# Loads of x for the residual stream tied to SyncE's weight loads, and the transposed x in five parts among the first weights

## The chip, the cores and the metric

The kernel runs on one core of a Trainium2 chip. The metric is the time of one execution on the device in microseconds (us), as the median of several runs. A profile of one execution stands beside it; its rows name the engines PE (TensorE), PEld (its weight loads), DVE (VectorE), ACT (ScalarE), POOL (GpSimd) and SP (SyncE).

## The reference

The kernel computes a decoder trunk of two layers over x, 256 positions by 2048 features, float32. Cut to what the change touches:

```python
def reference(x, ...):
    h = x
    for layer in range(DEPTH):                       # DEPTH = 2
        xn = rms_norm(h, norm_mix[layer])
        if layer % 2 == 0:
            mix = swa_mlstm_mixer(xn, w_in_even[0], w_out_even[0], ...)
        else:
            mix = forgetting_attention_mixer(xn, w_in_odd[0], ...)
        h = h + mix
        h = h + swiglu(rms_norm(h, norm_ffn[layer]), w_gate[layer], w_up[layer], w_down[layer])
    return rms_norm(h, norm_final)

def rms_norm(x, g):
    return x * rsqrt(mean(x * x, axis=-1) + 1e-5) * g

def swa_mlstm_mixer(xn, w_in, ...):
    proj = xn @ w_in                                 # 2048 features to all heads' inputs
    q_s, k_s, v_s, q_m, k_m, v_m, o_m, i_m, f_m = split_cols(proj, EVEN_SIZES)
    ...
```

The row factor rsqrt(mean(x * x) + 1e-5) scales a whole row of `xn`, so the kernel multiplies x times the gain g with the weights and applies the row factor to the product.

## The kernel before

All weights are float32 in DRAM. A product of float32 quality is made of three matmuls in PE's faster float32 form: each operand is split into a rounded part and the rest (`hi` and `lo` of a weight, `xh` and `xl` of x), and hi times xh, lo times xh and hi times xl are added up in PSUM (lines 178 to 180 of `gemm`).

Weights come in chunks: `load_raw` (line 105) issues on SyncE a load of 256 rows by 512 columns, 512 KB, into a tile `raw`, of which there are four buffers. `split_chunk` casts it on ACT into `hi` (line 150) and subtracts on DVE for `lo` (line 151); `hi` and `lo` have six buffers each. A chunk feeds 12 matmuls: two row blocks of 128, two halves of the 256 positions, three products. A raw buffer is free for the next load when `lo` is made.

The order of work at the start is this:

1. x is loaded a first time, transposed on the host, as `xc` (16 tiles of 128 features by 256 positions, 2 MB), in four loads of four tiles (line 115). Among them stand the loads of the first four chunks, kept in the list `ahead`.
2. The first projection, into `acc0`, are the keys and values of the window attention (512 columns at `OFF_KS`): chunks 1 to 8. For each n of four, the scalings of four tiles of `xc` to `xh` (ACT, line 562) and `xl` (DVE, line 563) stand ahead of two chunks.
3. The second projection, into `acc1`, is the first half of the queries: chunks 9 to 16. After every two chunks the kernel loads a quarter of x in its plain layout into `h`, the residual stream (line 573, 512 KB on SyncE), and ACT squares it and adds up the rows (line 201 in `square_sum`, two instructions per quarter, each with a read of the accumulator).
4. `rstd` makes of the sums the row factor `r` (DVE lines 207 and 208, POOL line 210). It is first used to take `acc0` out of PSUM: `kd` on ACT (line 604), `vs` on DVE (line 609). `acc0` and `acc1` hold two PSUM banks each, out of four in their pool; the third projection takes the banks of `acc0`.

The program isn't executed in the order it is written in: a scheduler places the instructions of each engine by its own estimate of times, under the data dependences, and every engine then executes its list in order. `tc.issue_after(ins)` adds an edge to this: what is traced in its block, on the engine of `ins`, is placed behind `ins`. In the loop of the second projection `ins` is `latest[0]`, the last cast on ACT, while the instruction in the block is a load on SyncE:

```python
        with tc.issue_after(latest[0].ins):
            nc.sync.dma_start(h[:, :, n * NB : (n + 1) * NB], xv[:, :, n * NB : (n + 1) * NB])
        square_sum("m0", n)
```

In the built program the head of SyncE's list, which holds all loads of weights, of `xc` and of `h`, reads: `xc` part 1, chunks 1 and 2, `xc` part 2, chunks 3 and 4, `xc` parts 3 and 4, `h` in four parts, chunks 5 to 24. ACT's list reads, from the first scaling on: four scalings, casts 1 and 2, four scalings, casts 3 and 4, eight scalings, eight squares, seven casts, `kd`, a cast, `kd`, casts.

Of the kernel before, what the change touches and what calls it, by code (L numbers as in the profile page):

```python
# [23 lines left out]
NB = 512  # L24
# [7 lines left out]
OFF_QS, OFF_KS = 0, 1024  # L32
# [22 lines left out]
def trunk(  # L55
# [20 lines left out]
    nc = tc.nc  # L76
# [22 lines left out]
    xc = gp.tile([P, KT, S], F32, name="xc")  # L99
    gT = cp.tile([P, 4 * KT], F32, name="gT")  # L100
    nc.scalar.dma_start(gT, gains)

    def load_raw(w, k0, c0, n, pool=wr):
        raw = pool.tile([P, CK, NB], F32, tag="raw", name="raw", bufs=4 if pool is wr else RAWS)
        nc.sync.dma_start(
            raw[:, :, 0:n], w[k0 * P : (k0 + CK) * P, c0 : c0 + n].rearrange("(k p) n -> p k n", p=P)
        )
        return raw

    wi = w_in_even[0]  # L110
    h = cp.tile([P, NT, D], F32, name="h")
    xv = x[0].rearrange("(t p) d -> p t d", p=P)
    ahead = []
    for n in range(4):
        nc.sync.dma_start(xc[:, 4 * n : 4 * n + 4, :], xt[:, 4 * n : 4 * n + 4, :])
        for k in {0: (0, 2), 1: (4, 6)}.get(n, ()):
            ahead.append(load_raw(wi, k, OFF_KS, NB))

    ident = cp.tile([P, P], F32, name="ident")
    nc.gpsimd.memset(ident, 0.0)  # L120
# [20 lines left out]
    latest = [None]  # L141

    def load_chunk(w, k0, c0, n):
        raw = ahead.pop(0) if ahead else load_raw(w, k0, c0, n)
        return split_chunk(raw, n)
# [18 lines left out]
    def gemm(acc, lhs, w, c0, n, k_from, k_to, k_all, skew=1):  # L164
        k0 = k_from
        while k0 < k_to:
            last = k_to == k_all and k0 + skew * CK >= k_all
            chunks = [load_chunk(w, kc, c0, n) for kc in range(k0, k_all if last else k0 + CK, CK)]
            order = [(i, t) for i in range(len(chunks) * CK) for t in range(NT)]
            if last:  # L170
                order.sort(key=lambda it: it[1])
            for i, t in order:
                k = k0 + i
                hi, lo = (c[:, i % CK, 0:n] for c in chunks[i // CK])
                ah, al = lhs(k)
                ts = slice(t * P, (t + 1) * P)
                o = acc[t][:, 0:n]
                nc.tensor.matmul(o, ah[:, ts], hi, start=(k == 0), stop=False)  # L178
                nc.tensor.matmul(o, ah[:, ts], lo, start=False, stop=False)  # L179
                nc.tensor.matmul(o, al[:, ts], hi, start=False, stop=(k == k_all - 1))  # L180
            k0 += len(chunks) * CK
# [14 lines left out]
    def square_sum(key, n):  # L196
        if n == 0:
            sums[key] = sm.tile([P, NT, 4], F32, tag="ss", name="ss")
        for t in range(NT):
            junk = sm.tile([P, NB], BF16, tag="junk", name="junk", bufs=1)  # L200
            nc.scalar.activation(
                junk, h[:, t, n * NB : (n + 1) * NB], AF.Square, accum_out=sums[key][:, t, n : n + 1]
            )
# [160 lines left out]
    def pair_group(fp, par, lhs, sums, mats, order, todo=()):  # L364
# [5 lines left out]
        for pos, (kind, pair) in enumerate(order):  # L370
# [18 lines left out]
            if first:  # L389
                prods = [bank(1 - par, "prod") for _ in range(4)]  # L390
            ra, rb = (load_raw(w, k0, c0, NB, fp) for w, c0 in mats)
            hg, lg = split_chunk(ra, NB)
            run_due(todo, pos)
# [175 lines left out]
    acc1 = new_acc()  # L569
    for n in range(4):  # L570
        gemm(acc1, x_of, wi, OFF_QS, NB, 4 * n, 4 * n + 4, KT)
        with tc.issue_after(latest[0].ins):
            nc.sync.dma_start(h[:, :, n * NB : (n + 1) * NB], xv[:, :, n * NB : (n + 1) * NB])
        square_sum("m0", n)
    r = rstd("m0")
    with tc.tile_pool(name="ev", bufs=1) as ev:
# [22 lines left out]
        with tc.tile_pool(name="sw", bufs=1) as sw:  # L599
# [10 lines left out]
            ks = sw.tile([P, KVH, S], F32, name="ks")  # L610
# [379 lines left out]
```

## Time and profile before

| | us |
|---|---|
| median of 3 runs | 2132.34 |
| lowest and highest | 2132.19, 2133.31 |
| the profiled execution | 2132.55 |
| its span, first to last instruction | 2130.8 |
| PE busy in it | 2108.0 |
| ACT busy, DVE busy | 1252.5, 1709.9 |

The granted clock of PE has a mean of 0.997 over the span. The DMA queues moved 420.95 MB, at a mean of 198 GB/s. Busy time of PE has modelled ends: a matmul of 512 columns is shown with some 0.39 us, and the next one of its kind begins 0.23 us after it.

### The profile page before, as it was taken

What the parts mean: (1) busy time and instruction counts of PE and PEld (TensorE: products, weight loads), DVE (VectorE), ACT (ScalarE), POOL (GpSimd) and SP (SyncE); (2) the same over time, 40 slices, a digit from 0 to 9 for tenths busy, and PEclk for the clock granted to TensorE, in tenths of its full rate; (3) what the DMA queues carried; (4) which work ended last, traced back from release to release, by engine and by line L of the source; (5) the groups of instructions that cost most, each with busy time, mean ns of one, the idle gap of its engine ahead of it and who ended that gap; (6) DMA issues with size and microseconds to landing.
All of it is one profiled execution on the core that took longest, in us unless ns stands there. A gap on an engine that the chain in (4) does not pass through costs nothing.

```text
span 2130.8 us, 26787 instructions
## 1 busy us (share of the span) xinstructions
PE 2108.0 (99%) x9708; PEld 1749.6 (82%) x9708; DVE 1709.9 (80%) x2204; ACT 1252.5 (59%) x1592; POOL 35.7 (2%) x61
## 2 busy tenths in 40 slices
PE   7999999999999999999999999999999999999998
PEld 5888888888888888888888888888888888888886
DVE  5666567899999999999755554668899998999995
ACT  6474456665577655766645444556655667556763
POOL 2010000000000000000000000000000000000000
PEclk9999999999999999999999999999999999999999
DMA  8455556675667666775575664656766767666763
GB/s 290 137 166 151 169 194 197 202 223 171 228 208 217 200 206 204 233 224 179 168 232 166 177 173 141 229 175 186 223 197 210 232 190 207 228 197 205 226 208 131
DMA packets 257845, 420.95 MB, mean 198 GB/s; under 512 B 56448, under 2 KB 64688, under 8 KB 257584
## 3 DMA queue, kind: packets, MB, share of 16 engines
q1 hardware_dynamic: 256832, 415.49, 62.9%
q0 software_dynamic: 736, 3.71, 0.6%
q8 instruction: 76, 1.25, 0.2%
q14 instruction: 57, 0.47, 0.1%
q10 hardware_dynamic: 144, 0.03, 0.0%
HBM read 406.57 MB, written 2.11 MB: 192 GB/s over the span
## 4 chain that ended last, share of the span: by engine, by line
PE 98%; DMA 1%; ACT 1%; DVE 0%; issue 0%; SPq 0%; DVEq 0%; POOLq 0%; POOL 0%; ACTq 0%
PE acc L357 17%; PE acc L358 17%; PE acc L359 17%; PE acc L180 11%; PE acc L178 11%; PE acc L179 10%; PE prod L357 4%; PE prod L358 4%; PE prod L359 4%; PE ptm L264 1%; PE p L281 1%; PE po L332 1%; DMA xc<-in_xt_dram 1%; PE pt L230 0%; PE pp L324 0%; PE p L274 0%
## 5 line engine op out<-in xcount | busy, mean ns | idle before, releaser
L150 ACT CAST hi<-raw 128x1024 fp32r<-128x1024 f32 (+2 forms) x682 | 696.0, 1032 | 584.5 <-PE acc L180 259.0
L151 DVE TENSOR_TENSOR lo<-raw,hi 128x1024 fp32r<-128x1024 f32 (+2 forms) x682 | 810.3, 1200 | 249.8 <-ACT hi L150 248.1
L358 PE MATMUL acc<-lo,xh 128*128 128x512 f32 x946 | 368.1, 389 | 0.0
L357 PE MATMUL acc<-hi,xh 128*128 128x512 f32 x946 | 365.1, 390 | 0.3 <-DVE u L422 0.3
L359 PE MATMUL acc<-hi,xl 128*128 128x512 f32 x946 | 363.2, 389 | 0.0
L178 PE MATMUL acc<-hi,xh 128*128 128x512 f32 (+3 forms) x736 | 276.5, 378 | 12.4 <-ACT hi L150 12.4
L180 PE MATMUL acc<-hi,xl 128*128 128x512 f32 (+3 forms) x736 | 277.2, 378 | 0.0
L179 PE MATMUL acc<-lo,xh 128*128 128x512 f32 (+3 forms) x736 | 276.7, 376 | 0.3 <-DVE lo L151 0.2
L357 PEld LDWEIGHTS acc<-hi,xh 128*128 128x128 f32 x946 | 177.6, 188 | 37.9 <-DVE u L422 1.1
L359 PEld LDWEIGHTS acc<-hi,xl 128*128 128x128 f32 x946 | 177.5, 188 | 37.1
L358 PEld LDWEIGHTS acc<-lo,xh 128*128 128x128 f32 x946 | 177.6, 188 | 36.6
L358 PE MATMUL acc<-lo,mh 128*128 128x512 f32 x444 | 173.1, 390 | 0.0
L359 PE MATMUL acc<-hi,ml 128*128 128x512 f32 x444 | 171.1, 389 | 0.0
L357 PE MATMUL acc<-hi,mh 128*128 128x512 f32 x444 | 170.1, 389 | 0.0
L178 PEld LDWEIGHTS acc<-hi,xh 128*128 128x128 f32 x736 | 139.6, 190 | 36.0 <-ACT hi L150 12.8
L179 PEld LDWEIGHTS acc<-lo,xh 128*128 128x128 f32 x736 | 139.6, 190 | 26.0 <-DVE lo L151 2.2
L180 PEld LDWEIGHTS acc<-hi,xl 128*128 128x128 f32 x736 | 139.5, 190 | 25.8 <-issue 1.9
L252 ACT CAST ht<-raw 128x1024 fp32r<-128x1024 f32 x94 | 98.7, 1050 | 51.8 <-issue 20.8
L253 DVE TENSOR_TENSOR lt<-raw,ht 128x1024 fp32r<-128x1024 f32 x94 | 114.6, 1219 | 16.5 <-ACT ht L252 16.2
L178 PE MATMUL acc<-hi,mh 128*128 128x512 f32 x320 | 125.8, 393 | 1.2 <-ACT mh L252 1.2
L179 PE MATMUL acc<-lo,mh 128*128 128x512 f32 x320 | 125.7, 393 | 0.0
L180 PE MATMUL acc<-hi,ml 128*128 128x512 f32 x320 | 124.0, 390 | 0.0
(307 smaller groups left out, 3071.6 us busy)
## 6 DMA issues: line engine op xcount, KB each, us to landing
raw<-in_w_gate_dram SPq DMA_DIRECT2D x176, 512.0 KB, 4.6
raw<-in_w_up_dram SPq DMA_DIRECT2D x176, 512.0 KB, 4.7
raw<-in_w_down_dram SPq DMA_DIRECT2D x176, 512.0 KB, 4.9
raw<-in_w_in_odd_dram SPq DMA_DIRECT2D x88, 512.0 KB, 3.8
raw<-in_w_in_even_dram SPq DMA_DIRECT2D x64, 512.0 KB, 4.4
raw<-in_w_out_even_dram SPq DMA_DIRECT2D x32, 512.0 KB, 3.7
raw<-in_w_out_odd_dram SPq DMA_DIRECT2D x32, 512.0 KB, 3.9
raw<-in_w_in_odd_dram SPq DMA_DIRECT2D x8, 272.0 KB, 2.9
```

The source lines that it names most:

```text
L150: latest[0] = nc.scalar.copy(hi[:, :, 0:n], raw[:, :, 0:n])
L151: nc.vector.tensor_tensor(out=lo[:, :, 0:n], in0=raw[:, :, 0:n], in1=hi[:, :, 0:n].bitcast(F32), op=ALU.subtract)
L178: nc.tensor.matmul(o, ah[:, ts], hi, start=(k == 0), stop=False)
L179: nc.tensor.matmul(o, ah[:, ts], lo, start=False, stop=False)
L180: nc.tensor.matmul(o, al[:, ts], hi, start=False, stop=(k == k_all - 1))
L252: nc.scalar.copy(dst_h, src)
L253: nc.vector.tensor_tensor(out=dst_l, in0=src, in1=dst_h.bitcast(F32), op=ALU.subtract)
L264: nc.tensor.transpose(pt[:, i, :], s_, ident)
L281: nc.tensor.matmul(p1[:, jj, :], q_of(j, 1), k_of(j), start=True, stop=True)
L357: nc.tensor.matmul(o, ah, hi, start=start, stop=False)
L358: nc.tensor.matmul(o, ah, lo, start=False, stop=False)
L359: nc.tensor.matmul(o, al, hi, start=False, stop=stop)
```

## The change

Two edits at the start of the kernel. `load_raw` now keeps its latest load in `load[0]`, and the loads of `h` name that load, an instruction of SyncE, in `issue_after`. The loads of `xc` become five: two tiles, two, four, four, four; chunk 1 stands behind the first part, chunk 2 behind the second, chunks 3 and 4 behind the third.

```diff
+    load = [None]
+
     def load_raw(w, k0, c0, n, pool=wr):
         raw = pool.tile([P, CK, NB], F32, tag="raw", name="raw", bufs=4 if pool is wr else RAWS)
-        nc.sync.dma_start(
+        load[0] = nc.sync.dma_start(
             raw[:, :, 0:n], w[k0 * P : (k0 + CK) * P, c0 : c0 + n].rearrange("(k p) n -> p k n", p=P)
         )
         return raw
...
     ahead = []
-    for n in range(4):
-        nc.sync.dma_start(xc[:, 4 * n : 4 * n + 4, :], xt[:, 4 * n : 4 * n + 4, :])
-        for k in {0: (0, 2), 1: (4, 6)}.get(n, ()):
-            ahead.append(load_raw(wi, k, OFF_KS, NB))
+    for k0, k1, ks in ((0, 2, (0,)), (2, 4, (2,)), (4, 8, (4, 6)), (8, 12, ()), (12, 16, ())):
+        nc.sync.dma_start(xc[:, k0:k1, :], xt[:, k0:k1, :])
+        ahead += [load_raw(wi, k, OFF_KS, NB) for k in ks]
...
     for n in range(4):
         gemm(acc1, x_of, wi, OFF_QS, NB, 4 * n, 4 * n + 4, KT)
-        with tc.issue_after(latest[0].ins):
+        with tc.issue_after(load[0].ins):
             nc.sync.dma_start(h[:, :, n * NB : (n + 1) * NB], xv[:, :, n * NB : (n + 1) * NB])
         square_sum("m0", n)
```

## The prediction

> **What bounds the kernel now.** I read the windows view first, over stretches that I cut at the idle ends of PE, then PE's waits, then the timeline of the first 34 us, then the landings of single loads.
>
> ```profile
> PE 2108.0 (99%) x9708; PEld 1749.6 (82%) x9708; DVE 1709.9 (80%) x2204; ACT 1252.5 (59%) x1592; POOL 35.7 (2%) x61
> PE acc L178 <- ACT hi L150: 12.4, 2, 7.5
> PE acc L178 <- ACT mh L252: 1.2, 1, 1.2
> 0.00:7.50 7.50, 0.00 (x0) 0.00 (x0) 1.75 (x6) 4.11 (x7) 3.51 (x14) 1.00 0.73 198
> 15.86:21.15 5.29, 5.29 (x22) 4.05 (x22) 4.25 (x9) 5.21 (x14) 0.96 (x3) 1.00 1.05 386
> 21.15:26.07 4.92, 0.00 (x0) 0.00 (x0) 0.54 (x3) 4.76 (x14) 4.50 (x12) 0.88 1.05 393
> 26.07:31.90 5.83, 5.79 (x13) 4.13 (x14) 4.72 (x5) 3.74 (x4) 3.41 (x4) 0.52 0.83 271
> 40.11:61.87 21.76, 21.76 (x98) 17.97 (x98) 12.55 (x12) 11.02 (x12) 0.00 (x0) 1.00 0.78 236
> 61.87:2120.00 2058.13, 2056.66 (x9509) 1709.45 (x9507) 1673.20 (x2155) 1212.41 (x1530) 22.24 (x29) 1.00 0.63 195
> ```
>
> A windows row gives the stretch, its length, then busy time and count of PE, PEld, DVE, ACT, POOL, then PEclk, DMA share, GB/s. PE is busy for 99% of the span; from 61.87 to 2120 us it lacks 1.47 us. So whatever PE gains before 62 us is kept to the end: what follows waits for PE. PE has two holes: 7.50 us at the start, and 4.92 us at 21.15. The second costs twice: the next stretch runs at a granted clock of 0.52. PE works chunk by chunk: a chunk is 512 KB of weights and 12 matmuls. Eight chunks (9 to 16) take 21.76 us undisturbed, 2.72 us each; chunk 5, in the stretch 26.07 to 31.90, takes 5.83.
>
> Why PE stands still at 21.15 is seen in the timeline (start, length, engine, line, in brackets the idle time before it):
>
> ```profile
> 4.81 1.70 ACT L562 ACTIVATE xh<-xc,gT 128x256 fp32r<-128x256 f32 x4 [2.10 <-DMA xc<-in_xt_dram]
> 5.12 7.13 SPq L573 DMA_DIRECT2D h<-in_x_dram  x4
> 6.42 1.03 ACT L150 CAST hi<-raw 128x1024 fp32r<-128x1024 f32 x1
> 7.48 1.23 DVE L151 TENSOR_TENSOR lo<-raw,hi 128x1024 fp32r<-128x1024 f32 x1 [0.45 <-ACT hi L150]
> 7.50 1.22 PE L178 MATMUL acc<-hi,xh 128*128 128x512 f32 x2 [7.50 <-ACT hi L150]
> 9.34 1.05 ACT L150 CAST hi<-raw 128x1024 fp32r<-128x1024 f32 x1 [1.89 <-DMA raw<-in_w_in_even_dram]
> 13.30 45.87 SPq L105 DMA_DIRECT2D raw<-in_w_in_even_dram  x20
> 13.52 2.12 ACT L150 CAST hi<-raw 128x1024 fp32r<-128x1024 f32 x2
> 14.58 2.36 DVE L151 TENSOR_TENSOR lo<-raw,hi 128x1024 fp32r<-128x1024 f32 x2 [0.46 <-ACT hi L150]
> 15.86 0.50 PE L179 MATMUL acc<-lo,xh 128*128 128x512 f32 x1 [0.21 <-DVE lo L151]
> 15.88 3.31 ACT L562 ACTIVATE xh<-xc,gT 128x256 fp32r<-128x256 f32 x8 [0.24 <-DMA xc<-in_xt_dram]
> 16.86 3.25 DVE L563 SCALAR_TENSOR_TENSOR xl<-xc,gT,xh 128x256 fp32r<-128x256 f32 x8
> 19.10 0.61 ACT L201 ACTIVATE junk<-h 128x512 bf16<-128x512 f32 x1
> 24.99 1.97 ACT L150 CAST hi<-raw 128x1024 fp32r<-128x1024 f32 x2
> 26.07 1.22 PE L178 MATMUL acc<-hi,xh 128*128 128x512 f32 x2 [4.93 <-ACT hi L150]
> ```
>
> SyncE issues the four loads of h (2 MB) from 5.12 on, and only then, from 13.30, the loads of chunks 5 and later. ACT squares h from 19.10 and casts chunk 5 only at 24.99. Two causes stand one behind the other: ACT's eight squares, and under them the weight, which lands late. The landings say how late (KB and us from issue to landing; the tile views of h and xc give min/median/max):
>
> ```profile
> L573 SPq DMA_DIRECT2D h<-in_x_dram x4: 368/863/1635, 5.1 to 11.9; - x4
> DMA to landing us min/median/max: 10.7/12.6/13.4
> L115 SPq DMA_DIRECT2D xc<-in_xt_dram x4: 395/500/553, 0.8 to 4.5; - x4
> DMA to landing us min/median/max: 3.9/10.8/12.6
> raw<-in_w_in_even_dram SPq DMA_DIRECT2D x1, 512.0 KB, 4.7
> raw<-in_w_in_even_dram SPq DMA_DIRECT2D x1, 512.0 KB, 10.6
> ```
>
> The loads of xc land from 0.8 + 3.9 = 4.7 to 4.5 + 12.6 = 17.1. Those of h land from 5.1 + 13.4 = 18.5 to 11.9 + 10.7 = 22.6, 1.36 us apart. Chunk 1 (issued at 1.26) lands at 6.0, chunk 5 (issued at 13.30, the last row) at 23.9.
>
> **The change, part by part.** The edge that should hold the loads of h back named a ScalarE copy and does nothing to SyncE's queue; it now names the last weight load. In the built instruction order the queue reads: two of the sixteen column tiles of xc, chunk 1, two tiles, chunk 2, four tiles, chunks 3 and 4, eight tiles in two loads, chunks 5 to 10, then h in four parts with two chunks between them. ACT's order has the eight scalings of xc followed by casts 5 to 10, then two squares after every two casts; DVE's follows suit. PE's order is the same but for a few swaps of neighbours, POOL's entirely.
>
> *Five parts of xc.* The first 2 MB on the queue (half of xc with chunks 1 and 2; then the second quarter) are the same bytes in another order, so every load from chunk 2 on lands as before. Only chunk 1 moves: it has 256 KB less ahead of it. At the 386 GB/s of the row above (a bound, as the queue ramps up here) that is 0.7 us: 6.0 becomes 5.3. The first part of xc, 256 KB shorter too, lands 0.7 us before 4.7, and ACT has only two scalings to do before the cast (4 take 1.70), ending by about 5.0, so the cast runs 5.4 to 6.45 and PE starts at 6.5 instead of 7.5. One load more on SyncE costs one issue, 0.4 to 0.55 us (row of xc), under the transfers that run meanwhile; were that cover gone it would be 0.5 us. But the 1.0 us isn't kept. Chunk 2 is cast at 9.34 as before and chunk 3 from 13.52, since their loads land as before; its lo is ready at 15.8. PE, ahead by 1.0, waits for chunk 3: some 0.6 us for hi and 0.8 for lo. From 15.86 on all is as before. Bounds: 0 to 1.0 us; I take 0, as the 15.86 row already waits for lo.
>
> *Loads of h behind chunk 10.* Chunks 5 to 8 take the places of the four loads of h, which have the same 512 KB: landing at about 18.5, 19.9, 21.2 and 22.6. Their issues wait for one of four raw buffers, freed by the lo of chunks 1 to 4: the fourth at 14.58 + 2.36 = 16.9, so each is issued before its place comes up. ACT ends the scalings at 15.88 + 3.31 = 19.2, casts chunk 5 until 20.2, chunk 6 until 21.3, chunk 7 until 22.3, chunk 8 by 23.7. DVE ends xl at 16.86 + 3.25 = 20.1 and has the lo of chunk 5 at 21.5 (1.23 us each), then one per 1.23 us. PE ends chunk 4 at 21.0 as before: hi is there, and two matmuls later, at 21.45, lo is 0.1 us away. The hole of 4.92 shrinks to 0.1, and chunk 5 runs at full clock.
>
> *The squares and what waits for them.* They cost ACT the same time as before (19.10 to 24.99, 1.5 us a pair), now among casts; per two chunks 2 x 1.05 + 1.5 = 3.6 us of ACT against PE's 5.44. A load of h that comes late would hold the casts behind it in ACT's order, but when ACT comes to the first pair, near 28.5, it has cast chunks 9 and 10 and PE is in chunk 6 or 7: 8 us of cover. On SyncE two chunks stand behind each load of h; its 1.36 us of transfer per 5.44 us fits, as the weights use 236 GB/s (row 40.11) where the queue has carried 386 to 393. The row scale r, which needs all the squares, comes near 42 instead of 29; its first user kd frees the banks of the first projection by about 45, wanted when PE ends chunk 16 near 54. That is 9 us of cover; with it gone, each us is lost whole.
>
> **The sum.** Hole: 4.92 - 0.1 = 4.8. Chunk 5: 5.83 - 2.72 = 3.1. Five parts: 0. End of hole and chunk 5 together: before, chunk 6 starts at 31.90; after, at 21.0 + 0.1 + 2.72 = 23.8. That is 8.1 against 4.8 + 3.1 = 7.9 (PE's modelled end at 21.15 lies 0.15 behind its last issue); I take 8.0. The profiled execution took 2132.55 us, 1.75 more than its span of 2130.8; less 8.0 is **2124.5**. The median of the three runs, 2132.34, lies 0.2 below, so it says the same.
>
> One row bears on the clock, in the stage of small matmuls, with no wait near it, and one rule:
>
> ```profile
> 195.50:199.00 3.50, 3.50 (x12) 2.80 (x11) 1.82 (x3) 2.41 (x6) 0.00 (x0) 0.51 0.02 5
> ```
>
> The Trainium skill, page "TensorE: Matmul & The Clock Gate", section "HAM oscillation — how this bites in real kernels" says that a wait over its window of about 3.4 us brings the clock to half; the trace agrees, with 0.52 behind the 4.92 us hole and 1.00 behind the 0.21 us wait. Its section "A second HAM failure mode: psum-queue depth-cycling" holds that short idle times between groups of matmuls can do that too: that would speak against the new waits, and is the first rival; by the first section the sum stays, by the second it would be about 2126.2.
>
> **The rivals.**
>
> *The clock falls at the new waits.* PE's 0.6 and 0.8 us near 14 to 16 may share a stretch in which the clock is set, just after the start. One stretch at half costs 3.50 x 0.49 = 1.7 us (row 195.50): 2126.2. For it: 1.4 us of idleness in 3.4 us is much more than the 0.21 that the trace shows harmless. Against: the start has a hole of the same kind already (two matmuls at 7.50, the next when lo is ready at 8.71) and the clock rises all the same. Chance 0.10.
>
> *Another wait takes the hole's place.* Chunks 5 to 8 come as late as the raw buffers let them, or the small transfers spread into the new order, and half of the gain goes: a hole of about 2.5 us, and, as the clock may fall again, 1.5 us more. 2132.55 - 4 = 2128.5. For it: four buffers only. Against: the fourth is free at 16.9, 6 us before its place. If the load order didn't change what PE waits for at all, 2132.4; the built order speaks against that. Chance of both 0.08, "no change" by my bound.
>
> *Slower: the squares hold the casts.* If loads of h, behind weights in one queue, took the 13.4 us of the row above again, ACT would stand at each pair of squares: a round of h, squares and two casts takes up to 13.4 + 1.5 + 2.1 = 17 us, against 5.44 for PE. Three later rounds lose 11.6 each, 35 us less the 8 us of cover and the 8.0 gained: some 2151. It decides from the point where a load of h lands over 5.44 - 3.6 + 8 = 10 us after its issue in the first round, and less in later ones. For it: one in-order queue. Against: those 13.4 us had up to eight 512 KB loads ahead of them; behind 28 us only four raw buffers and one or two parts of h can be on the way. Chance 0.04.
>
> **How the numbers follow.** Forecast 0.78, with its own range of 2123.0 (start gain kept: -1.0, and 0.5 for the clock's phase) to 2125.6 (1.1 us of waits at chunks 5 to 8, taken as the one wait of 1.2 us that remains elsewhere); clock rival 0.10 at 2126.2, to 2126.8; no change 0.08; slower 0.04. The range 2122.9 to 2126.8 holds the first two, 0.88. A measurement of this kernel can tell 0.2% (4.3 us) from no change. Faster by more: 0.88; within: 0.08; slower: 0.04.
>
> **What would show it.** Right: PE's first matmul near 6.5; chunk 3's lo still near 15.9 with PE waiting before it; no PE wait over 0.5 us between 16 and 60; a PEclk of 1.00 from 21 to 60; chunk 16 ending near 53.8 instead of 61.87; loads of h in under 7 us. Wrong: a PE wait on hi between 20 and 54, a PEclk near 0.5 there, a wait of the next projection for kd, or an end of chunk 16 as proposed with a later stretch that gives it back.

## The result

The changed kernel took 2125.90 us (median of 7 runs, 2124.63 to 2127.21), the kernel before 2132.27 (7 runs, 2131.60 to 2133.31): 6.4 us less, a ratio of 0.997 with a 95% interval of 0.9958 to 0.9981. Its profiled execution took 2125.90 us, with a span of 2124.2, against 2132.55 and 2130.8.

PE's waits in the profile after (engine, line, released by: us in total, times, longest):

```profile
PE acc L179 <- ACT hi L151: 7.1, 1, 7.1
PE acc L179 <- ACT mh L253: 1.2, 1, 1.2
PE acc L180 <- DVE lo L152: 0.9, 2, 0.5
PE acc L358 <- DVE u L423: 0.9, 2, 0.5
```

The first line counts one wait where the kernel before had two: the start is left, the hole of 4.92 us is gone. Two short waits for `lo` and two for `u` are new or longer. The windows view, cut at PE's waits (columns as in the prediction):

```profile
0.00:7.08 7.08, 0.00 (x1) 0.00 (x1) 0.96 (x4) 3.42 (x5) 3.51 (x14) 1.00 0.67 183
7.08:16.38 9.30, 8.31 (x27) 5.55 (x27) 6.28 (x10) 5.65 (x9) 0.00 (x0) 1.00 1.01 337
16.38:21.49 5.11, 5.11 (x22) 4.23 (x23) 5.05 (x10) 5.08 (x10) 0.79 (x3) 1.00 0.99 366
21.49:24.37 2.88, 2.88 (x14) 2.18 (x12) 2.88 (x3) 2.21 (x3) 2.88 (x4) 1.00 0.72 169
...
32.50:54.30 21.80, 21.80 (x98) 17.98 (x97) 14.50 (x16) 16.24 (x26) 0.72 (x1) 1.00 0.93 321
```

From 16.38 to 54.30 us PE is never idle. Chunk 5 runs from 21.49 to 24.37 at a granted clock of 1.00: 2.88 us instead of 5.83. The timeline of the start, with the casts and their waits:

```profile
5.98 1.04 ACT L151 CAST hi<-raw 128x1024 fp32r<-128x1024 f32 x1 [0.30 <-DMA raw<-in_w_in_even_dram]
...
7.08 1.22 PE L179 MATMUL acc<-hi,xh 128*128 128x512 f32 x2 [7.08 <-ACT hi L151]
...
10.42 1.05 ACT L151 CAST hi<-raw 128x1024 fp32r<-128x1024 f32 x1 [1.45 <-DMA raw<-in_w_in_even_dram]
...
12.78 0.50 PE L180 MATMUL acc<-lo,xh 128*128 128x512 f32 x1 [0.42 <-DVE lo L152]
...
14.03 2.15 ACT L151 CAST hi<-raw 128x1024 fp32r<-128x1024 f32 x2
...
16.38 0.50 PE L180 MATMUL acc<-lo,xh 128*128 128x512 f32 x1 [0.53 <-DVE lo L152]
...
19.62 1.98 ACT L151 CAST hi<-raw 128x1024 fp32r<-128x1024 f32 x2
...
30.06 0.63 ACT L202 ACTIVATE junk<-h 128x512 bf16<-128x512 f32 x1 [0.39 <-DMA h<-in_x_dram]
...
46.22 1.27 ACT L605 ACTIVATE kd<-acc,r 128x512 f32<-128x512 f32 x2 [0.30 <-POOL r L211]
...
54.29 1.03 PE L265 MATMUL ptm<-ident,kd 128*128 128x128 f32 x8
```

The last row is a mark for all that follows: the first transposes of kd stand right behind chunk 16 in PE's order. Before, they began at 61.71. So 7.4 us are won there; at the end of the span 6.6 are left.

### The profile page after: what moved, and what is told of

Its sections match the earlier page's. It is cut to its first block, busy times and chain, and to the rows that moved or that the text cites. A ratio compares the mean times of both kernels' runs of the same rounds, so it can differ in the third digit from the quotient of the medians.

```text
span 2124.2 us, 26790 instructions
## 1 busy us (share of the span) xinstructions
PE 2105.4 (99%) x9708; PEld 1747.6 (82%) x9708; DVE 1709.8 (80%) x2204; ACT 1252.2 (59%) x1592; POOL 39.6 (2%) x61
## 4 chain that ended last, share of the span: by engine, by line
PE 97%; DMA 1%; DVE 1%; ACT 0%; issue 0%; SPq 0%; DVEq 0%; POOLq 0%; POOL 0%; ACTq 0%
PE acc L358 17%; PE acc L359 17%; PE acc L360 17%; PE acc L181 11%; PE acc L180 11%; PE acc L179 11%; PE prod L359 4%; PE prod L358 4%; PE prod L360 4%; PE ptm L265 1%; PE p L282 1%; PE po L333 1%; PE pt L231 0%; DMA raw<-in_w_up_dram 0%; DMA xc<-in_xt_dram 0%; PE pp L325 0%
## 5 line engine op out<-in xcount | busy, mean ns | idle before, releaser
L254 DVE TENSOR_TENSOR lt<-raw,ht 128x1024 fp32r<-128x1024 f32 x94 | 114.6, 1219 | 16.6 <-ACT ht L253 16.2
```

What stands on the lines that cost most here:

```text
L254: nc.vector.tensor_tensor(out=dst_l, in0=src, in1=dst_h.bitcast(F32), op=ALU.subtract)
```

## The experiments

The "mark" below is that start of the transposes of kd. Times are medians, with the number of runs; beside these kernels, the kernel before had medians of 2131.9 to 2132.3. The two medians of the changed kernel are 1.5 us apart, so smaller differences between kernels are read from the marks and the traces, not from the medians.

| kernel | mark | PE's first matmul of the projection | lo of chunk 3 is ready | time |
|---|---|---|---|---|
| before | 61.71 | 7.50 | 15.81 | 2132.3 (7) |
| changed | 54.29 | 7.08 | 16.32 | 2125.9 (7) |
| changed, again | 54.52 | 8.38 | 16.43 | 2124.4 (5) |
| tie alone | 54.22 | 7.72 | 15.84 | 2125.4 (6) |
| tie alone, again | 54.23 | 7.54 | 15.56 | 2125.0 (5) |
| five parts alone | 60.61 | 6.60 | 16.00 | 2130.9 (11) |
| squares behind casts | 61.01 | 7.53 | 15.80 | 2131.3 (10) |
| spare matmuls in the hole | 59.78 | 7.58 | 16.02 | 2130.1 (10) |
| changed, small loads late | 53.62 | 6.60 | 13.26 | 2125.0 (5) |
| tie, small loads late | 53.75 | 7.59 | 12.72 | 2124.9 (5) |
| changed, late, warmed | 51.40 | 6.65 | 13.47 | 2122.3 (5) |
| changed, warmed | 54.84 | 6.69 | 16.05 | 2125.4 (5) |
| tie, late, warmed | 51.94 | 7.47 | 12.74 | 2122.6 (5) |

**The tie alone.**

```diff
-        with tc.issue_after(latest[0].ins):
+        with tc.issue_after(load[0].ins):
             nc.sync.dma_start(h[:, :, n * NB : (n + 1) * NB], ...)
```

> Only the tie: loads of h behind chunk 10, xc in four parts as before. My theory (the tie makes the whole gain, the five parts cost some 0.5 us, because their smaller first loads and the tiny loads of POOL collide and chunk 3 lands later): PE starts at 7.5 as before, lo of chunk 3 is ready at 15.8 and not at 16.3, chunk 5 starts near 21.0, chunk 16 ends near 53.8 (the changed kernel's first transpose of kd stands 7.4 us earlier than before, here 8.0); time 2125.4 or less, 0.5 under the changed kernel. Rival (the five parts bring 0.4 us by the earlier start and chunk 3's landing is chance): chunk 16 ends no earlier than in the changed kernel, at 54.3 or later, time 2126.0 to 2126.5.

The tie has the whole gain: 0.997 (0.9958 to 0.9981), the mark at 54.22. Chunk 3's lo is 0.5 us earlier than in the changed kernel, as expected (the reason given, a collision with POOL's loads, falls below), but chunk 5 isn't earlier: it came at 21.6. Here the clock rose late. PE's timeline shows it by the distance of the matmuls, 0.43 and then 0.23 us:

```profile
12.56 0.63 PE L181 MATMUL acc<-lo,xh 128*128 128x512 f32 x1
12.98 0.58 PE L182 MATMUL acc<-hi,xl 128*128 128x512 f32 x1
...
13.86 0.39 PE L181 MATMUL acc<-lo,xh 128*128 128x512 f32 x1
14.10 0.39 PE L182 MATMUL acc<-hi,xl 128*128 128x512 f32 x1
```

PE was slow until 13.4 us, 5.7 us after its start; in the kernel before until 11.2, 3.7 us after it. Chunks 1 and 2 took until 16.1, and chunk 3's lo was there already.

**Five parts alone.** The edge names the ScalarE copy again.

> Only the five parts; the edge of h names the ScalarE copy again. The built order then has h in three parts, chunk 5, the fourth part, and six of the eight squares ahead of cast 5. My theory: PE starts near 7.1, chunk 3's lo comes near 16.3 as in the changed kernel, PE stands still from 21.5 until cast 5 is done behind six squares, near 25.2, and the clock falls again: some 0.5 to 1 us faster than before only through the two squares that the scheduler moved, 2131.3 to 2132.5. Rival (the five parts make a good share of the gain): 2129 or less, with the hole under 2 us.

A miss by 0.4 us in the time (2130.9), and PE started at 6.60 instead of 7.1; right in the kind:

```profile
21.36:24.74 3.38, 0.00 (x0) 0.00 (x0) 0.02 (x1) 3.29 (x10) 3.16 (x9) 0.90 1.05 388
24.74:30.80 6.06, 6.02 (x13) 4.35 (x14) 3.99 (x6) 4.35 (x8) 4.65 (x7) 0.50 1.00 353
```

The hole is there, shorter by the two squares that this kernel's scheduler moved, and the clock falls behind it. The ratio is 0.9995 (0.9986 to 1.0004), not told from no change.

**The squares moved, the loads of h not.**

```diff
-        square_sum("m0", n)
+        with tc.issue_after(latest[0].ins):
+            square_sum("m0", n)
```

> As before, but the squares are placed behind the casts of the second projection; the loads of h stay ahead of chunk 5. It parts the two causes of the hole. My theory (the squares stand over a weight that lands late): cast 5 starts when chunk 5 lands, near 23.9 instead of 24.99; the hole shrinks from 4.9 to 3.9 us, the clock still falls, time 2131.2. Rival (the squares on ACT are the cause, the place of the loads is not): no hole, a gain of 7 us or more, 2125.

The timeline of ACT, and the rows of the windows view with the hole and with chunk 5 behind it:

```profile
15.71 3.31 ACT L562 ACTIVATE xh<-xc,gT 128x256 fp32r<-128x256 f32 x8 [0.22 <-DMA xc<-in_xt_dram]
23.77 1.04 ACT L150 CAST hi<-raw 128x1024 fp32r<-128x1024 f32 x1 [4.75 <-DMA raw<-in_w_in_even_dram]
```

```profile
21.17:24.87 3.70, 0.01 (x1) 0.00 (x1) 0.02 (x1) 1.04 (x1) 3.42 (x10) 0.97 1.05 386
24.87:31.00 6.13, 5.96 (x13) 4.27 (x14) 4.60 (x4) 3.71 (x4) 3.63 (x5) 0.50 0.98 349
```

With nothing of its own to do, ACT waits 4.75 us for chunk 5's weights: the loads of h ahead of them account for 3.7 us of the hole, the squares only for the 1.2 on top, and the clock still falls. The time (2131.3, ratio 0.9996, 0.9987 to 1.0005) is not told from no change. The rival, a gain of 7 us, falls.

**Spare matmuls in the hole.** PE gets 22 matmuls between chunks 4 and 5, on `xh` alone.

> As before, with 22 spare matmuls of 512 columns on PE between chunks 4 and 5, on xh alone and into a PSUM tile that nothing reads: they fill the hole and keep PE busy. It measures what the clock costs by itself. My theory (of the 3.1 us by which chunk 5 is too long, about 2.35 is the clock and 0.76 the wait for lo): granted clock 1.00 from 21 to 32, chunk 5 takes about 3.5 us instead of 5.83, the first transpose of kd comes 2.1 to 2.4 us earlier, time 2130.0 to 2130.4. Rival (chunk 5 is long because weights come late): no gain, 2132.3 or more.

```profile
21.57 5.15 PE L574 MATMUL spare<-xh 128*128 128x512 f32 x22
26.55 0.61 PE L180 MATMUL acc<-hi,xh 128*128 128x512 f32 x2
27.45 0.50 PE L181 MATMUL acc<-lo,xh 128*128 128x512 f32 x1 [0.28 <-DVE lo L151]
...
29.85 0.62 PE L180 MATMUL acc<-hi,xh 128*128 128x512 f32 x2
```

```profile
21.10:27.20 6.10, 6.07 (x27) 4.70 (x25) 1.44 (x3) 5.74 (x14) 5.61 (x13) 1.00 1.05 391
27.20:32.00 4.80, 4.55 (x20) 3.78 (x21) 3.70 (x5) 2.74 (x3) 2.46 (x3) 1.00 0.71 227
```

The clock stays at 1.00, and chunk 5 takes 29.85 - 26.55 = 3.3 us instead of 5.83: 2.5 us of the loss is the clock, 0.6 the wait for lo. The spare matmuls run 0.5 us over, so the mark moves 1.9, a little less than expected. The median, 2130.1, is as expected, but its ratio of 0.9992 (0.9982 to 1.0001) isn't told from no change: the price of the clock is read from the trace.

**What holds up the first chunks.** POOL's four small loads, for gates and sinks, are issued behind `dist` (the same edit in the changed kernel and in the tie alone):

```diff
+        io = nc.gpsimd.iota(dist, ...)
+        with tc.issue_after(io.ins):
+            nc.gpsimd.dma_start(bias_g[:, 0:4], ...)      # and the three others, moved from the start
```

> The changed kernel with POOL's four small loads (biases and sinks, 20 KB in all, spread over 128 partitions) issued behind dist, near 20 us, instead of from 1.4 us on. It asks what delays the first chunks. My theory (these small loads hold up the 16 engines between 5 and 11 us, and that is why chunk 2 lands at 10.4 and chunk 3 at 13.8 for 1.5 and 2.5 MB): chunk 2 lands before 8.5, chunk 3 before 11.5, PE's waits for lo before chunks 2 and 3 go, chunk 5 starts between 20.0 and 21.0 instead of 21.49 (by the clock's phase), time 2124.5 to 2125.4. Rival (the queue's own start-up with 2 KB packets is the limit): chunk 3 lands at 13 or later and the time is that of the changed kernel, 2125.9.

> The tie alone, xc in four parts, with the same four small loads moved behind dist. My theory: chunk 1 and the start of PE as before (near 6.0 and 7.5), chunk 3 lands before 11.5, but as PE starts 0.4 us later than with five parts it gains less over the tie alone: chunk 5 starts between 20.5 and 21.5, time 2125.0 to 2125.6, some 0.4 us over the five parts with late small loads. Rival (as there): chunk 3 lands at 13 or later, time as for the tie alone, 2125.4.

First the changed kernel: its windows row from 4.5 to 10.5 us, and the small loads' queue in its first 12 us (packets, MB, share of the 16 engines' time). Then the same windows row with late small loads:

```profile
4.50:10.50 6.00, 3.38 (x7) 2.29 (x8) 2.99 (x5) 2.93 (x6) 0.00 (x0) 1.00 0.97 225
```

```profile
q0 software_dynamic: 128, 0.02, 16.6%
```

```profile
4.50:10.50 6.00, 3.87 (x8) 2.65 (x9) 4.26 (x7) 4.42 (x8) 0.00 (x0) 1.00 1.03 374
```

20 KB, 16 or 64 bytes for each of 128 partitions, take 16.6% of 12 us, 2 us of all 16 engines; without them the rate is 374 GB/s instead of 225, and chunk 3's lo comes 3 us earlier, at 13.26 and 12.72. The Trainium skill, page "DMA: Bandwidth & Descriptors", section "Specifications" says that transfers under 512 B fall short of the line rate; the trace agrees. The rival, that the queue's own start-up is the limit, falls: chunk 3 lands at 10.6 and 10.2 us instead of 13.7 and 13.1. But the mark moves only 0.5 to 0.9 us, and the medians (2125.0, 2124.9) can't be told from those without the edit. Both runs had the clock's late rise, at 13.2 and 12.5: with the weights there, PE is bound by its own start. The medians are 0.1 apart, where 0.4 was expected for the five parts. One thing stays with late small loads: with five parts chunk 3's lo comes 0.5 us later than with four.

**The same kernels again**, for the scatter.

> The changed kernel once more, for the scatter from run to run. My theory (two parts of the time are chance: the phase of the clock's stretches at the start, and waits of PE for single DVE sums later that depend on the landing of a weight): chunk 3's lo again near 16.1 to 16.4, chunk 5's start within 0.4 of 21.5, first transpose of kd 7.2 to 7.8 us earlier than before, later waits of PE on u between 0 and 1 us; median 2125.4 to 2126.4. Rival (the 0.9 us that the changed kernel's profile gives back behind 60 us is systematic): it gives back 0.8 us or more again, at the same two places.

> The tie alone once more. My theory (five parts cost about 0.5 us by the later chunk 3, where the clock rises early; where it rises late, as in the first run of the tie, that cost is hidden): chunk 3 lands near 13.1, chunk 5 starts between 21.0 (early rise) and 21.6 (late rise), median 2125.0 to 2125.6, 0.2 to 0.8 under the changed kernel of this call. Rival (the two can't be told apart): medians within 0.2 of each other.

The changed kernel was 1.5 us faster than the first time (2124.38, in 2122.82 to 2126.97), the tie alone 2124.98, so their order turned round; the expectations of 2125.4 to 2126.4 for the changed kernel, and of a lead of 0.2 to 0.8 for the tie, are missed. PE's waits behind 60 us in the changed kernel again, and in the tie again:

```profile
PE acc L179 <- ACT mh L253: 1.2, 1, 1.2
PE acc L358 <- DVE u L423: 0.3, 1, 0.3
```

```profile
PE acc L180 <- ACT mh L254: 1.2, 1, 1.2
```

0.3 and 0 us for u, instead of 0.9: what the changed kernel's first profile gave back is not systematic.

**PE warmed up.** Twelve (in the tie, fourteen) spare matmuls run on a tile of ones from 1.56 us on, while PE waits for chunk 1.

```diff
+    wz = gp.tile([P, NB], BF16, name="wz")
+    nc.vector.memset(wz, 1.0)
+    spare = pm.tile([P, NB], F32, tag="pm", name="spare")
+    for i in range(12):
+        nc.tensor.matmul(spare, wz[:, 0:P], wz, start=(i == 0), stop=(i == 11))
```

> The changed kernel with late small loads and 12 spare matmuls (bf16, 512 columns, on a tile of ones, into a PSUM tile that nothing reads) on PE from about 1.3 us on, while it waits for chunk 1. My theory (with the small loads out of the way the start is bound by the clock, which rises 3.4 to 6.8 us after PE begins): the clock rises before 8.2 us, chunk 1 is at full speed but for its first matmuls, chunk 5 starts between 18.2 and 19.2 instead of 20.98 in the kernel with late small loads alone, first transpose of kd near 51 to 52, time 2122.0 to 2123.3. Rival (PE's start is bound by landings, not by the clock): time within 0.5 of late small loads alone, 2124.5 to 2125.4.

> The changed kernel with the same 12 spare matmuls, its small loads early as before. My theory (with the small loads in the way chunk 3's landing is the bound, so the clock is worth little): chunk 3's lo at 16.0 to 16.5 again, PE waits longer before chunks 2 and 3, chunk 5 starts at 21.2 to 21.5, time 2124.8 to 2125.8, at most 0.5 under the changed kernel. Rival (the clock at the start is the bound here too): a gain of 1.5 us or more, 2123.5.

> The tie with xc in four parts, late small loads, and 14 spare matmuls ahead. It asks what the five parts are worth once neither the small loads nor the clock hides them. My theory (five parts start PE 0.9 us earlier, 6.6 against 7.5, and nothing else is late): chunk 5 starts 0.6 to 0.9 later than with five parts, 19.0 to 20.0, time 0.5 to 0.9 over it, 2122.8 to 2124.0. Rival (the five parts are worth nothing at all): the same within 0.3.

With late small loads the warmed kernel is the fastest of all: 2122.28 us, 0.9952 (0.9938 to 0.9965) of the kernel before, and 2.1 to 3.6 us under the changed kernel's two medians. Its chunk 1 waits only for data:

```profile
1.56 4.92 PE L104 MATMUL spare<-wz 128*128 128x512 bf16 x12 [1.56 <-DVE wz L101]
6.65 0.73 PE L180 MATMUL acc<-hi,xh 128*128 128x512 f32 x2 [0.18 <-ACT hi L152]
...
18.64 0.61 PE L180 MATMUL acc<-hi,xh 128*128 128x512 f32 x2
```

Chunk 5 starts at 18.64, inside the 18.2 to 19.2 expected. Here, with neither small loads nor clock in the way, the five parts are worth 51.94 - 51.40 = 0.5 us at the mark; chunk 5 of the tie starts at 19.29, 0.65 later, as expected. The medians are 0.3 apart, which can't be told from nothing. With the small loads early, warming brings nothing in the median (2125.44), chunk 5 starts at 22.20, later than the 21.2 to 21.5 expected, and something else shows:

```profile
6.56:9.97 3.41, 2.88 (x12) 1.97 (x12) 2.11 (x3) 0.98 (x3) 0.00 (x0) 1.00 0.96 233
9.97:13.39 3.42, 1.91 (x8) 0.97 (x7) 1.91 (x3) 2.28 (x5) 0.00 (x0) 1.00 1.02 383
13.39:16.80 3.41, 3.41 (x10) 2.63 (x9) 2.96 (x5) 3.13 (x6) 0.00 (x0) 0.50 1.03 408
```

PE, faster, waits longer for chunk 2, 0.98 us for hi and 0.53 for lo: 1.5 us of a stretch of 3.4. The next stretch runs at half clock. That is the prediction's first rival, in a kernel that differs from the changed one only by its warm PE; the mark comes 0.55 later than in the changed kernel.

## Why the prediction was right, and where it was off

The forecast of 2124.5 stands 1.4 under the first median and 0.1 over the second; the sign and the mechanism of the gain held. The first median lies in the stated range, but 0.3 above the forecast's own part of it (2123.0 to 2125.6) and nearer to the 2126.2 of the clock rival: the time alone would not have decided between them, the granted clock of 1.00 from 16.38 to 54.30 us does. Step by step:

- *The hole*: right. 4.8 us were to go, and behind 16.38 none is left. Chunk 5's weights now land before ACT comes to them (8.31 + 10.7 = 19.0, 18.5 forecast); the cast begins at 19.62 (19.2 forecast), and PE needs no wait for its lo. The two causes stood in the order told: the weights were the deeper one.
- *Chunk 5's clock and wait*: right. 3.1 us were to go, 2.95 went (5.83 to 2.88); the spare matmuls put 2.5 of it on the clock.
- *Squares, r and kd*: right. The loads of h make ACT wait 1.6 us in all and PE not at all. The row scale came later than forecast, kd at 46.2 to 47.5 and vs until 48.3 instead of 45, which leaves 6 us of the cover of 9. The loads took longer than the "under 7 us" of the signs, up to 8.6:

```profile
L574 SPq DMA_DIRECT2D h<-in_x_dram x4: 462/464/498, 23.7 to 36.5; - x4
...
  DMA h<-in_x_dram: 1.6, 4
...
DMA to landing us min/median/max: 6.3/7.1/8.6
```

- *Five parts*: the step that failed. It said that chunk 1 lands 0.7 us earlier, that all later chunks land as before, and that the issue of one load more is covered by the transfers that run meanwhile. The landings after, of chunks 1, 2 and 3 (KB and us from issue to landing):

```profile
raw<-in_w_in_even_dram SPq DMA_DIRECT2D x1, 512.0 KB, 4.7
raw<-in_w_in_even_dram SPq DMA_DIRECT2D x1, 512.0 KB, 8.2
raw<-in_w_in_even_dram SPq DMA_DIRECT2D x1, 512.0 KB, 10.4
```

  Chunk 1 took the same 4.7 us as before with 256 KB less ahead of it, so the first matmul came at 7.08, not 6.5; in the second profile it took 6.0 us, and the first matmul came at 8.38. In the other four kernels with five parts it took 4.2 to 4.3 us (4.7 to 5.0 with four parts), and PE started at 6.60 to 6.69, as forecast. Why the changed kernel itself missed this twice is left open. Chunks 2 and 3 land late wherever there are five parts: chunk 2 at 2.24 + 8.2 = 10.4 instead of 9.3, chunk 3 at 3.34 + 10.4 = 13.7 instead of 13.2. SyncE's issues of chunks 3 and 4, before and then after:

```profile
2.78 1.14 SPq L105 DMA_DIRECT2D raw<-in_w_in_even_dram  x2
```

```profile
3.34 2.40 SPq L107 DMA_DIRECT2D raw<-in_w_in_even_dram  x2
```

  Chunk 3 is issued 0.56 us later, behind one load more, and takes 10.4 us to its landing in both kernels: the later issue comes through whole. So the cover wasn't there, and the 0.5 us that the prediction named for that case is near what was paid. POOL's small loads lengthen chunk 3's way in both orders alike (7.4 to 7.7 us without them, 10.1 to 10.4 with them); they are not what parts five from four. With them early, chunk 3's lo comes at 16.0 to 16.4 with five parts and at 15.6 to 16.0 with four; with them late, at 13.3 and 13.5 against 12.7. That the late issue is the whole cause is read from these landings; no run changes the issue alone, and chunk 2 is later by more than its own 0.5 us. At the mark the changed kernel loses only 0.1 to 0.3 us to the tie, because the tie's clock rose late in both its profiles: that the term of 0 nearly came true is luck.
- *The sum*: 8.0 forecast, 7.4 and 7.2 at the mark. The missing 0.6 is the later chunk 3 in one profile and a late start with a late clock in the other; of the 0.8 lost behind the mark in the first, 0.6 are the longer waits for u. The second profile loses nothing there.
- *The rivals*: the clock didn't fall at the new waits (0.42 and 0.53 us, 0.95 in all, less than the 1.28 that left it up in the warmed tie, below); in the warmed kernel 1.5 in one stretch brought it down, so its chance was not given for nothing. No other wait took the hole's place. Nothing of the slower rival was seen.

## What to carry to other kernels

The ordering edge of this scheduler did nothing to a load on another engine's queue than the one it named: look in the built order of the queue whether an edge holds. A transfer that isn't wanted yet, ahead of weights in the one queue that feeds PE, took its own time here, and then the clock's once more; the deepest wait is found by moving the visible one away. At the start of a kernel look at what is small and in many pieces, and keep PE warm while it waits, but do both: at the mark, both together brought 2.9 to 3.1 us over the changed kernel, the first alone 0.9 or less, the second alone nothing. A load split in two costs one issue more, here some 0.5 us to all that stands behind it in the queue.

## What the runs showed of the hardware that was not expected

- The clock needs no whole stretch of idleness to fall. In the warmed kernel 1.91 us busy of 3.42 halved it (rows of 9.97 and 13.39 above), while in the warmed tie 2.13 busy of 3.41, with 1.28 idle, did not. The Trainium skill, page "TensorE: Matmul & The Clock Gate", section "HAM oscillation — how this bites in real kernels", gives waits of over about 3.4 us as what brings it down; here 1.5 did. Where the border lies the runs don't show. The rows of the warmed tie:

```profile
4.52:7.93 3.41, 2.13 (x10) 0.89 (x8) 2.16 (x5) 3.01 (x6) 0.00 (x0) 1.00 1.03 399
7.93:11.34 3.41, 2.89 (x13) 2.17 (x12) 3.41 (x6) 3.19 (x6) 0.00 (x0) 1.00 1.05 404
```

- The rise comes 3.0 to 6.6 us after PE's first matmul (4.52 - 1.56 in the warmed tie, 13.2 - 6.6 in the changed kernel with late small loads); two profiles of the changed kernel itself have 3.4 and 4.9. What sets it the runs don't show. The windows view has no record before the first rise and shows 1.00 there; only the distance of the matmuls tells.
- In the stage of small matmuls near 190 us one stretch at half clock comes and goes: none with the squares moved, two in the warmed kernel with late small loads, at some 1.7 us each (half of 3.4). Runs of one kernel differ by up to 5 us, more than the terms disputed here, and the mean granted clock goes with the time: in the warmed kernel with early small loads, two runs at 0.999 took 2122.5 and 2122.9 us, three at 0.997 took 2125.4 to 2127.8. That stretches like these make that difference is likely, but not shown, as only one run of each was profiled.

The row with the squares moved, then the one of the warmed kernel with late small loads:

```profile
185.00:200.00 15.00, 15.00 (x77) 12.25 (x78) 9.95 (x24) 7.59 (x15) 0.00 (x0) 1.00 0.33 91
```

```profile
183.40:190.20 6.80, 6.80 (x21) 5.18 (x20) 4.10 (x9) 3.51 (x9) 0.00 (x0) 0.50 0.15 55
```
